# Two row tiles cast first and transposed in bfloat16 on TensorE, with a new plan of the first ten units

## The chip, the cores and the metric

The kernel runs on one core of a Trainium2 chip. The metric is the device time of one execution in microseconds. Most executions agree within 0.3%, and the times here are medians. A ratio compares two kernels in the same rounds, so it is not quite the ratio of the medians beside it; its 95% interval stands in brackets. A profile is one execution, and its span is some 2 us shorter than the time.

## The reference

```python
def reference(x, w1, w2):            # x: 16 x 512 x 1024, w1 and w2: 1024 x 768, float32
    y1 = np.matmul(x, w1)
    y2 = np.matmul(x, w2)
    return (np.tanh(y1) * y2).astype(np.float32)
```

The 8192 rows of x are 64 row tiles of 128. A matmul needs each row tile transposed, with the 1024 columns on the partitions.

## The kernel before

The first six row tiles, "the head", are multiplied in bfloat16 while the weights are still arriving. The other 58 tiles form 29 pairs. Each pair is multiplied with each weight ("a unit", 58 of them) in float16 by seven products of half-size blocks in place of eight; a product is four matmuls of 384 columns, p1 to p7. Tiles of the pairs are transposed by DMA, tiles of the head on TensorE.

```python
    def pe_transpose_f(mt, h):                       # float32, half a tile
        for k in range(KH):
            pin(nc.tensor.transpose(banks[6 + h][:, k * P:(k + 1) * P],
                                    hf[mt][:, (h * KH + k) * P:(h * KH + k + 1) * P], ident))

    def evacuate_f(mt, h, eng):                      # PSUM float32 -> SBUF bfloat16, half a tile
        ...
    def pe_transpose_b(mt, bank):                    # bfloat16, a whole tile: half the PSUM bytes
        b = bank.bitcast(bf16)
        for k in range(KO):
            pin(nc.tensor.transpose(b[:, k * P:(k + 1) * P], hb[mt][:, k * P:(k + 1) * P], ident_b))
```

The start and the first ten units follow a fixed plan: one list of names per engine, and each engine works its list strictly in order. In the names, `T` is a transpose, `e` its evacuation (the copy from PSUM, where TensorE writes, to SBUF), `hx` the cast of a head tile, `m20F3` the 512-column matmul of tile 2 with weight 0 (w1) and slice 3 (`G`: the other 256 columns), `ca3`/`cb3` the cast of slice 3 of w1/w2, `ax`, `rx`, `cx`, `Tx` the absolute-sum, scale, cast and DMA transpose of a tile of a pair, `s1` to `s4` sums of blocks of x and `t1` to `t4` sums of blocks of a weight, `seed` a copy between two PSUM banks, and `p5.0` product 5 of unit 0. From unit 10 on, a formula gives each operation its place.

```python
    for mt in range(4):
        for h in range(2):
            op(f"T{mt}{h}", "pe", 0.45, 4.5 + 2.3 * mt + 0.1 * h, [f"Lx{mt}", f"e{mt - 1}{h}" if mt else ""], pe_transpose_f, mt, h)
            op2("e", f"e{mt}{h}", ("dve", "act")[h], ...)
    ...
            at(slot(z - 30 + 4 * h), abs_x, i, h)            # steady part: absolute-sums of a pair
        late = 1.1 * (i == FIRST + 1)
        at(slot(z - 25 + late), scale_x, i)
        for h in range(2):
            at(slot(z - 24 + (1 + h) * late + 4 * h), cast_x, i, h, "dve")
            at(slot(z - 24 + (1 + h) * late + 4 * h), transpose_x, i, h)
```

## Time and profile before

| kernel before | |
|---|---|
| time, median of 4 runs | 316.13 us (315.47 to 316.74) |
| span of the profiled run | 314.2 us |
| TensorE, VectorE, ScalarE busy | 98%, 78%, 73% |
| a product of four 384-column matmuls, start to start | 0.65 us |

The chain of waits and TensorE's timeline stand in the prediction below. What they do not show is why TensorE loses 0.74 us at the handoff. These lines are of VectorE's timeline of the kernel before (start, length, instruction, idle before it and what ended it):

```profile
42.48 0.69 DVE L287 TENSOR_TENSOR o<-o,bank 128x512 f32<-128x512 f32 x1 [1.06 <-PE bank L270]
43.09 0.42 DVE L382 TENSOR_TENSOR s<-xT 128x512 f16<-128x512 f16 x1
...
44.77 1.82 DVE L318 SCALAR_TENSOR_TENSOR t<-wf,wp1r,b 128x1536 f16<-128x1536 f32 x1
```

VectorE sat idle for 1.06 us in front of the last head multiplication, because that needs TensorE's last head group. Sums of x and t1 of w2 (line L318) stood behind it in the list, and the product that needs t1 started at 46.63, when t1 was done.

### The profile page before, as it was taken

The numbers are of one execution on the slowest core, as the hardware profiler recorded it, in microseconds if no ns is written. First come the engines' busy times: TensorE is split into PE (matmuls) and PEld (weight loads), VectorE is DVE, ScalarE is ACT, GpSimd is POOL, SyncE is SP. The second block draws the span as 40 slices with busy tenths as digits, with TensorE's granted clock in tenths as the row PEclk, the third lists the DMA queues.
The fourth block names the chain that finished last, engine by engine and source line by source line (L and its number), as shares of the span: only waits on it lengthen the run. The fifth ranks groups of instructions, "written<-read, shape, count | busy, mean of one in ns | idle before, by whom it ended". The sixth has DMA issues, their size and how long they took to land.

```text
span 314.2 us, 5489 instructions
## 1 busy us (share of the span) xinstructions
PE 307.3 (98%) x1893; PEld 185.6 (59%) x1898; DVE 244.8 (78%) x571; ACT 230.5 (73%) x453; POOL 4.3 (1%) x10
## 2 busy tenths in 40 slices
PE   7999999999999999999999999999999999999995
PEld 5756656666656555555555556555555555555662
DVE  1688988888788778877777887777788777778653
ACT  3798879787888777778777777877777787776552
POOL 0000000000000000000000000000000000000004
PEclk9999999999999999999999999999999999999999
DMA  7999398999999999999999989999998989985322
GB/s 276 407 399 381 78 310 237 271 299 258 290 288 310 297 272 231 228 294 266 285 240 252 273 253 225 291 252 259 253 251 281 260 256 271 237 256 126 144 103 100
DMA packets 82300, 80.59 MB, mean 256 GB/s; under 512 B 63584, under 2 KB 64096, under 8 KB 82272
## 3 DMA queue, kind: packets, MB, share of 16 engines
q1 hardware_dynamic: 81552, 78.46, 88.0%
q10 hardware_dynamic: 720, 1.77, 1.4%
q8 instruction: 15, 0.25, 0.3%
q14 instruction: 13, 0.11, 0.1%
HBM read 39.85 MB, written 25.17 MB: 207 GB/s over the span
## 4 chain that ended last, share of the span: by engine, by line
PE 89%; DMA 8%; DVE 1%; issue 1%; ACT 0%; ACTq 0%; SPq 0%; DVEq 0%
PE bank L401 84%; DMA wf<-in_w_dram 8%; PE bank L267 3%; PE bank L270 2%; DVE t L318 1%; DVE s L382 1%; PE bank L238 0%; DVE o L437 0%; ACT o L283 0%; ACTq L250 0%; SPq L250 0%; ACT junk L260 0%; PE bank L300 0%; DVE o L287 0%; DVE out_r L390 0%
## 5 line engine op out<-in xcount | busy, mean ns | idle before, releaser
L401 PE MATMUL bank<-t,s 128*128 128x384 f16 x696 | 131.5, 326 | 0.4 <-DVE t L318 0.4
L401 PEld LDWEIGHTS <-s 128*128 128x128 f16 x928 | 90.7, 98 | 61.1 <-issue 0.8
L401 PEld LDWEIGHTS <-xT 128*128 128x128 f16 x696 | 68.0, 98 | 46.7 <-issue 0.9
L401 PE MATMUL bank<-b,xT 128*128 128x384 f16 x464 | 93.7, 326 | 0.0
L423 DVE TENSOR_TENSOR c<-bank,u 128x384 f32<-128x384 f32 x58 | 31.9, 553 | 41.1 <-PE bank L401 39.6
L340 ACT ACTIVATE junk<-x_f 128x1024 bf16<-128x1024 f32 x58 | 60.8, 1049 | 2.4 <-DMA x_f<-in_x_dram 2.4
L431 ACT ACTIVATE th<-c,out_r 128x384 f32<-128x384 f32 x58 | 35.3, 609 | 21.1 <-DVE c L423 21.1
L401 PE MATMUL bank<-b,s 128*128 128x384 f16 x232 | 47.0, 326 | 0.0
L401 PE MATMUL bank<-t,xT 128*128 128x384 f16 x232 | 46.9, 325 | 0.0
L418 ACT ACTIVATE u<-bank 128x384 f32<-128x384 f32 x58 | 28.2, 487 | 20.0 <-PE bank L401 19.7
L360 DVE TENSOR_SCALAR x_h<-x_f,pr 128x1024 f16<-128x1024 f32 x55 | 41.0, 746 | 0.2
L431 ACT ACTIVATE th<-bank,out_r 128x384 f32<-128x384 f32 x58 | 33.3, 574 | 6.1 <-PE bank L401 6.1
L414 ACT ACTIVATE bank<-bank 128x384 f32<-128x384 f32 x58 | 27.9, 481 | 12.6 <-DVE o L437 10.0
L437 DVE SCALAR_TENSOR_TENSOR o<-bank,out_r,th 128x384 f32<-128x384 f32 x58 | 35.4, 610 | 2.0 <-PE bank L401 2.0
L423 DVE TENSOR_TENSOR c<-bank,s 128x384 f32<-128x384 f32 x58 | 32.1, 554 | 6.1 <-PE bank L401 5.0
L437 DVE SCALAR_TENSOR_TENSOR o<-c,out_r,th 128x384 f32<-128x384 f32 (+1 forms) x57 | 34.3, 606 | 0.4 <-ACT th L431 0.2
L418 ACT ACTIVATE s<-bank 128x384 f32<-128x384 f32 x58 | 27.9, 482 | 7.3 <-PE bank L401 5.1
L382 DVE TENSOR_TENSOR s<-xT 128x512 f16<-128x512 f16 x58 | 24.0, 416 | 0.2
L267 PE MATMUL bank<-wb,xTb 128*128 128x512 bf16 x91 | 23.6, 379 | 0.1
L270 PE MATMUL bank<-wb,xTb 128*128 128x256 bf16 x96 | 14.6, 273 | 0.1
L260 ACT ACTIVATE junk<-wf 128x768 bf16<-128x768 f32 (+1 forms) x13 | 12.8, 988 | 1.4 <-DMA wf<-in_w_dram 1.2
L267 PEld LDWEIGHTS <-xTb 128*128 128x128 bf16 x96 | 9.3, 99 | 7.5 <-DVE xTb L231 0.3
(49 smaller groups left out, 143.4 us busy)
## 6 DMA issues: line engine op xcount, KB each, us to landing
x_f<-in_x_dram SPq DMA_DIRECT2D x64, 512.0 KB, 5.8
out_dram<-o SPq DMA_DIRECT2D x62, 384.0 KB, 3.6
wf<-in_w_dram SPq DMA_DIRECT2D x12, 384.0 KB, 7.7
wf<-in_w_dram ACTq DMA_DIRECT2D x4, 384.0 KB, 8.5
xT<-x_h SPq DMA_TRANSPOSE x58, 3.7
out_dram<-o SPq DMA_DIRECT2D x3, 192.0 KB, 1.9
out_dram<-o ACTq DMA_DIRECT2D x1, 192.0 KB, 1.9
```

What stands on the lines that cost most here:

```text
L260: pin(nc.scalar.activation(junk[:, :n * N].rearrange("p (k n) -> p k n", n=N), w_f[t][:, k:k + n, :], ACT.Abs, accum_out=asum_w[t][:, j:j ...
L267: pin(nc.tensor.matmul(bank, hx[mt][:, k, :], w_b[t][k][:, :F], start=k == 0, stop=k == KO - 1))
L270: pin(nc.tensor.matmul(bank[:, at_:at_ + G], hx[mt][:, k, :], w_b[t][k][:, F:], start=k == 0 and mt % 2 == 0, stop=k == KO - 1, skip_group ...
L340: pin(nc.scalar.activation(junk[:, :K], xs[HEAD + 2 * i + h], ACT.Abs, scale=2.0 ** -12, accum_out=pair_sum[i][:, h:h + 1]))
L360: pin(nc.vector.tensor_scalar(xh, xs.pop(mt), pair_r[i][:, h:h + 1], None, ALU.mult))
L382: pin((nc.vector if eng == "dve" else nc.gpsimd).tensor_tensor(s, st[i, a], st[i, b], op))
L401: pin(nc.tensor.matmul(bank[:, cols], st[i, a][:, k, :], wt[t][b][:, k, cols], start=start and k == 0, stop=stop and k == KH - 1, skip_gro ...
L414: pin(nc.scalar.activation(ub[u]["b"][:, :Q], ub[u]["a"][:, :Q], ACT.Copy))
L418: pin(nc.scalar.activation(c, ub[u][bank][:, :Q], ACT.Copy))
L423: pin(nc.vector.tensor_tensor(c, ub[u][bank][:, :Q], ub[u][other], ALU.add))
L431: pin(nc.scalar.activation(th, v, ACT.Tanh, scale=rs[i][:, 0, h:h + 1]))
L437: pin(nc.vector.scalar_tensor_tensor(o[:, h, q * Q + cols.start:q * Q + cols.stop], v, rs[i][:, 1, h:h + 1], tanhs[i, h, q][:, cols], ALU. ...
```

## The change

Its intent: on TensorE a bfloat16 transpose costs half of a float32 one (56 against 109 ns from start to start, as the prediction reads it from the trace), so two more of the head's tiles are cast before the transpose; and the plan is made anew around this.

```diff
-    for mt in range(4):
+    for mt in range(2):
         for h in range(2):
             op(f"T{mt}{h}", "pe", 0.45, ..., pe_transpose_f, mt, h)
             ...
+    for mt in (2, 3):
+        op2("hx", f"hx{mt}", "dve", 4.5 + 2.3 * mt, [f"Lx{mt}", "hx2" if mt == 3 else ""], cast_head_x, mt)
+        op(f"T{mt}", "pe", 0.45, 4.6 + 2.3 * mt, [f"hx{mt}", f"e1{mt - 2}"], pe_transpose_b, mt, banks[4 + mt])
+        op2("eb", f"e{mt}1", "dve", 4.7 + 2.3 * mt, [f"T{mt}", "e10" if mt == 2 else "e21"], evacuate_b, mt, banks[4 + mt])
     ... (needs and buffers that name these operations follow)
-    FILL = {"m00F0": 3, "m00F1": 6}
+    FILL = {"T10": 9, "m00G1": 3}
     "pe":                               (the start, the first matmuls with w2, the handoff)
-    T00 T01 m00F0 m00G0 T10 T11 ... m10F0 T20 m10G0 m10G1 m10F1 T21 m20G0 ... T30 T31 m10G3
+    T00 T01 T10 T11 m00G0 m00F0 ... m10F1 T2 m00G2 m00F2 m10F2 m10G2 m20G0 ... m20G2 T3 m10G3
-    ... m00F5 m00F6 m00F7 suma m11F0 m20F6 m20F7 m01F0 ... m30F7 m21F0 m21F1 m11F2 ...
+    ... suma m11F0 m01F0 m31F0 m11F1 ... m01F3 m21G3 m31F3 m11F3 m21F0 m00F3 m00F4 m00F5 m00F6 m00F7 ...
-    ... m51F7 p1.0 p1.1 p5.0 p6.0 p2.0 ...
+    ... m51G5 p1.0 p1.1 p5.0 p5.1 p2.0 p6.0 p6.1 m41G3 m41G4 m41G5 m41G6 m41G7 p7.0 ... m51G6 m51G7 ...
     "act":
-    ... tanh4G ax20 cx11 b11b b22b ...                   u2.8 f01.6 s5.8 cx61 s5.9 seed.9 f10.8 seed.10 ...
+    ... b11b ax20 tanh4G b22b ...                        f11.6 seed.9 f00.8 ... u2.9 s5.10 seed.10 f00.10
     "dve":
-    ... mul4G s1.0 s2.0 s4.0 s3.0 sx1 t1b ...
+    ... t1b s1.0 t2b s2.0 rx2 s3.0 ... mul4G ...
     "dma":
-    ... Lb5 Lb6 Lx5 Lb7 Lp00 ...
+    ... Lb5 Lx5 Lb6 Lp00 Lb7 ...                         (cuts marked by dots; the lists are long)
```

More of the change, by code (lines that the diff above doesn't have):

```diff
@@ L58 @@
     ELSEWHERE = {
-        "e01": "dve", "e11": "dve", "e20": "act", "e21": "dve", "e31": "dve", "ca0": "act", "ca1": "act",
-        "cb4": "act", "b22a": "dve", "cx11": "act", "cx31": "act", "cx61": "act"
+        "e00": "act", "e11": "dve", "ca1": "act", "b22a": "dve", "cx11": "act", "cx31": "act", "cx41":
+        "act", "cx60": "act"
     }
-    FILL = {"m00F0": 3, "m00F1": 6}
+    FILL = {"T10": 9, "m00G1": 3}
     ORDER = {
         "pe": """
-            T00 T01 m00F0 m00G0 T10 T11 m00F1 m00G1 m10F0 T20 m10G0 m10G1 m10F1 T21 m20G0 m20F0 m20F1 m20G1
-            m10G2 m20G2 m00F2 m00G2 m20F2 m10F2 T30 T31 m10G3 m00G3 m20F3 m10F3 m20G3 m00F3 m10F4 m10G4 m20F4
-            m20G4 m00G4 m00F4 m30G0 m30G1 m30G2 m30G3 m20G5 m10G5 m10F5 m20F5 m20G6 m10G6 m10F6 m30G4 m30G5
-            m30G6 m20G7 m10G7 m30G7 m10F7 m00F5 m00F6 m00F7 suma m11F0 m20F6 m20F7 m01F0 m00G5 m00G6 m00G7
-            m11F1 m01F1 m30F0 m30F1 m30F2 m30F3 m30F4 m30F5 m30F6 m30F7 m21F0 m21F1 m11F2 m21F2 m01F2 m11F3
-            m21F3 m01F3 m31F0 m31F1 m31F2 m31F3 m21G0 m21G1 m21G2 m21G3 m31G0 m31G1 m31G2 m31G3 m01F4 m31G4
-            m21G4 m11F4 m01G0 m01G1 m11G0 m11G1 m01G2 m01G3 m01G4 m31F4 T4 m11F5 m11F6 m01F5 m31F5 m01G5 m01G6
-            m31F6 m01F6 m31G5 m31G6 m01F7 m31F7 m11F7 m31G7 T5 m40F0 m40F1 m40F2 m40F3 m40F4 m40F5 m40F6 m01G7
-            m40F7 m21G5 m21G6 m50F0 m50F1 m50F2 m50F3 m50F4 m50F5 m50F6 m50F7 m21F4 m21F5 m21G7 m21F6 m21F7
-            m11G2 m11G3 m11G4 m11G5 m11G6 m11G7 m40G0 m50G0 m50G1 m50G2 m50G3 m50G4 m50G5 m50G6 m50G7 m40G1
-            m40G2 m40G3 m40G4 m40G5 m40G6 m40G7 sumb m41F0 m41F1 m41F2 m41F3 m41F4 m41F5 m41F6 m41F7 m41G0
-            m41G1 m41G2 m41G3 m41G4 m41G5 m41G6 m51G0 m51G1 m51G2 m51G3 m51G4 m51G5 m51G6 m51G7 m41G7 m51F0
-            m51F1 m51F2 m51F3 m51F4 m51F5 m51F6 m51F7 p1.0 p1.1 p5.0 p6.0 p2.0 p3.0 p7.0 p5.1 p6.1 p4.0 p2.1
-            p7.1 p1.2 p3.1 p4.1 p1.3 p6.2 p2.2 p5.2 p6.3 p2.3 p5.3 p7.2 p7.3 p3.2 p4.2 p3.3 p4.3 p1.4 p1.5
-            p5.4 p5.5 p2.4 p6.4 p6.5 p2.5 p7.4 p7.5 p3.4 p3.5 p4.4 p4.5 p1.6 p1.7 p5.6 p6.6 p2.6 p6.7 p2.7
-            p7.6 p3.6 p5.7 p7.7 p4.6 p3.7 p1.8 p4.7 p1.9 p2.8 p6.8 p5.8 p5.9 p7.8 p1.10 p3.8 p4.8 p3.9 p6.9
-            p2.9 p2.10 p7.9 p5.10 p4.9
@@ new lines @@
+            T00 T01 T10 T11 m00G0 m00F0 m00G1 m00F1 m10F0 m10G0 m10G1 m10F1 T2 m00G2 m00F2 m10F2 m10G2 m20G0
+            m20G1 m20F0 m20F1 m20F2 m20G2 T3 m10G3 m00G3 m10F3 m20F3 m20G3 m20F4 m00G4 m20G4 m10G4 m30F0 m30F1
+            m30G0 m30G1 m30G2 m30G3 m30G4 m20F5 m00G5 m10G5 m30G5 m20G5 m20F6 m00G6 m30G6 m20G6 m10G6 m20F7
+            m20G7 m30G7 m00G7 m10G7 m10F4 m10F5 m10F6 m10F7 suma m11F0 m01F0 m31F0 m11F1 m31F1 m01F1 m21G0
+            m21G1 m31G0 m11F2 m31F2 m01F2 m21G2 m01F3 m21G3 m31F3 m11F3 m21F0 m00F3 m00F4 m00F5 m00F6 m00F7
@@ new lines @@
+            m21F1 m21F2 m21F3 m30F2 m30F3 m30F4 m30F5 m30F6 m30F7 T4 m01G0 m01G1 m01G2 m11G0 m11G1 m11G2 m11G3
+            m21F4 m21F5 m11F4 m31F4 m01F4 m01F5 m21G4 m11F5 m31F5 m01G3 m01G4 m01G5 m21F6 m11F6 m31F6 m01F6
+            m01G6 m11G4 m11G5 m11G6 m01F7 m11G7 m21F7 m31F7 m01G7 m11F7 T5 m40F0 m40F1 m40F2 m40F3 m40F4 m40F5
+            m40F6 m40F7 m50F0 m50F1 m50F2 m50F3 m50F4 m50F5 m50F6 m50F7 sumb m40G0 m21G5 m21G6 m21G7 m31G1
+            m31G2 m31G3 m31G4 m31G5 m31G6 m31G7 m41F0 m41F1 m41F2 m40G1 m40G2 m41F3 m41F4 m41F5 m41F6 m41F7
@@ new lines @@
+            m40G3 m40G4 m40G5 m50G0 m40G6 m40G7 m50G1 m50G2 m50G3 m50G4 m50G5 m50G6 m50G7 m51F0 m51F1 m51F2
+            m51F3 m51F4 m51F5 m51F6 m51F7 m41G0 m51G0 m41G1 m41G2 m51G1 m51G2 m51G3 m51G4 m51G5 p1.0 p1.1 p5.0
+            p5.1 p2.0 p6.0 p6.1 m41G3 m41G4 m41G5 m41G6 m41G7 p7.0 p3.0 p7.1 p4.0 m51G6 m51G7 p3.1 p2.1 p4.1
+            p1.2 p1.3 p5.2 p5.3 p2.2 p6.2 p6.3 p2.3 p7.2 p7.3 p3.2 p4.2 p3.3 p4.3 p1.4 p5.4 p1.5 p6.4 p2.4
+            p5.5 p6.5 p2.5 p3.4 p7.4 p7.5 p5.6 p4.4 p3.5 p4.5 p1.6 p1.7 p5.7 p2.6 p6.6 p3.6 p6.7 p2.7 p1.8
@@ L82 @@
+            p7.6 p7.7 p3.7 p4.6 p4.7 p5.8 p5.9 p6.8 p2.8 p3.8 p1.9 p7.8 p3.9 p5.10 p4.8 p6.9 p2.9 p1.10 p7.9
+            p2.10 p4.9
         """,
         "act": """
-            ca0 absa0 ca1 absa1 e20 absa2 absa3 absa4 absa5 absa6 absa7 tanh2G absb0 tanh1F tanh0G tanh2F cb4
-            tanh0F absb2 absb6 tanh3F absb4 ax00 absb7 ax01 b21a tanh4F tanh5F ax10 ax11 tanh4G ax20 cx11 b11b
-            b22b seed.0 seed.1 s5.0 u2.0 ax21 b21b u2.1 f00.0 s5.1 f10.0 ax31 seed.2 ax30 seed.3 f11.0 u2.2
@@ L87 @@
-            u2.3 s5.2 s5.3 f00.2 f01.0 ax40 cx31 f10.2 seed.4 ax41 seed.5 s5.4 s5.5 u2.4 u2.5 f11.2 f00.4 ax51
-            f01.2 ax50 f10.4 seed.6 f11.4 seed.7 f01.4 u2.6 s5.6 ax61 u2.7 s5.7 f00.6 f11.6 f10.6 seed.8 ax60
-            f00.8 u2.8 f01.6 s5.8 cx61 s5.9 seed.9 f10.8 seed.10 u2.9 f01.8 f11.8 f00.10 s5.10
+            e00 e01 ca1 absa1 absa0 absa2 absa3 absa4 absa5 absa6 absa7 tanh2G tanh0G tanh2F tanh1F absb0 b21a
+            tanh0F absb2 tanh3F absb4 ax00 absb6 ax01 absb7 tanh4F ax10 tanh5F ax11 b11b ax20 tanh4G b22b ax21
@@ L90 @@
+            seed.0 seed.1 s5.0 cx11 u2.0 u2.1 s5.1 b21b f00.0 f10.0 ax30 ax31 seed.2 seed.3 f01.0 ax40 u2.2
+            f11.0 u2.3 s5.2 s5.3 ax41 f00.2 f10.2 cx31 seed.4 s5.4 seed.5 ax51 u2.4 u2.5 f01.2 f11.2 s5.5 cx41
+            s5.6 f00.4 f01.4 f10.4 seed.6 ax50 seed.7 f00.6 f11.4 u2.6 u2.7 s5.7 ax60 ax61 f01.6 f10.6 seed.8
+            s5.8 cx60 u2.8 s5.9 f11.6 seed.9 f00.8 f01.8 f11.8 f10.8 u2.9 s5.10 seed.10 f00.10
         """,
         "dve": """
-            e00 e01 e10 e11 ca2 e21 ca3 ca4 e30 ca5 ca6 e31 ca7 parta cb0 cb1 scalea b11a cb2 cb3 t1a b22a hx4
@@ L93 @@
-            cb6 cb5 t2a e41 cb7 hx5 mul0F mul3F mul1F e51 t3a rx0 cx00 cx01 mul2G mul2F mul0G partb t4a rx1
-            cx10 scaleb mul4F sx0 mul4G s1.0 s2.0 s4.0 s3.0 sx1 t1b t2b t3b c22.0 rx2 sx2 cx20 t4b s1.1 c22.1
-            f00.1 s2.1 c12.0 f10.1 s3.1 cx21 c12.1 s4.1 f11.1 rx3 cx30 c22.2 c22.3 s3.2 s1.2 f00.3 f01.1 c12.2
-            c12.3 s2.2 f10.3 mul5F rx4 cx40 s4.2 cx41 s3.3 c22.4 f11.3 c22.5 f00.5 s1.3 c12.4 f01.3 s2.3 f10.5
-            rx5 f11.5 s4.3 cx50 c12.5 f01.5 c22.6 sx3 cx51 c22.7 f00.7 s1.4 s2.4 sx4 s3.4 c12.6 c12.7 rx6 cx60
@@ L98 @@
-            s4.4 sx5 f01.7 c22.8 f10.7 f11.7 s1.5 s2.5 c12.8 s3.5 c12.9 f00.9 c22.9 s4.5 f11.9 f01.9 f10.9
+            ca0 e10 e11 hx2 ca2 e21 hx3 ca3 ca4 e31 ca5 ca6 ca7 parta cb0 cb1 scalea cb2 cb3 b11a b22a hx4 cb5
+            cb4 t1a t2a cb6 e41 cb7 hx5 mul0F mul1F e51 rx0 mul2F cx00 partb t4a scaleb cx01 mul2G mul3F mul4F
+            rx1 mul0G cx10 t1b s1.0 t2b s2.0 rx2 s3.0 sx0 t3a s4.0 t3b c22.0 cx20 c22.1 t4b c12.0 f00.1 f10.1
+            s1.1 c12.1 cx21 s2.1 f01.1 s4.1 rx3 s3.1 cx30 f11.1 c22.2 c22.3 sx1 s1.2 c12.2 s2.2 f00.3 c12.3
@@ L99 @@
+            f10.3 rx4 s4.2 sx2 s3.2 mul4G cx40 mul5F s1.3 c12.4 c22.4 f11.3 sx3 c22.5 f01.3 f00.5 c12.5 s2.3
+            f01.5 f10.5 s4.3 rx5 s3.3 cx50 f11.5 cx51 c12.6 c22.6 c22.7 sx4 s1.4 c12.7 s2.4 s3.4 rx6 s4.4
+            f10.7 f00.7 f01.7 c12.8 s1.5 c22.8 f11.7 cx61 s3.5 s2.5 sx5 s4.5 f00.9 c12.9 c22.9 f11.9 f01.9
+            f10.9
         """,
         "dma": """
-            Lx0 La0 Lx1 La1 Lx2 La2 Lx3 La3 La4 La5 La6 La7 Lb0 Lb1 Lb2 Lb3 Lb4 Lx4 Lb5 Lb6 Lx5 Lb7 Lp00 Lp01
-            Lp10 Lp11 Tx00 Lp20 Tx01 st3 Lp21 Tx10 Lp30 st4 Tx11 Lp31 st1 Tx20 Lp40 Lp41 Tx21 st2 Lp50 Tx30
@@ L103 @@
-            Lp51 Tx31 Lp60 st5 Tx40 Lp61 st0 Tx41 Lp70 store1.5 Tx50 store0.5 Lp71 Tx51 store0.1 store1.1 Tx60
-            store0.7 store1.7 Tx61 store1.3 store0.3 store0.9 store1.9
+            Lx0 La0 Lx1 La1 Lx2 La2 Lx3 La3 La4 La5 La6 La7 Lb0 Lb1 Lb2 Lb3 Lb4 Lx4 Lb5 Lx5 Lb6 Lp00 Lb7 Lp01
+            Lp10 Lp11 Tx00 Lp20 Tx01 Lp21 st1 Lp30 Tx10 Lp31 Tx11 Lp40 st0 Tx20 Lp41 st2 Tx21 Lp50 Tx30 Lp51
+            store1.1 Tx31 Lp60 st4 Tx40 st5 Lp61 Tx41 Lp70 store0.5 st3 Tx50 store1.5 store0.1 Tx51 Lp71 Tx60
@@ L105 @@
+            store0.7 store1.7 Tx61 store0.3 store1.3 store0.9 store1.9
         """,
@@ L547 @@
                 op(f"abs{a}{k}", "act", 0.23 + 0.82 * n, 8 + 1.3 * k + 17 * t, [f"L{a}{k + n - 1}"], abs_w, t, k, n)
-    held = {6: "e30", 7: "e31"}
+    held = {6: "e21", 7: "e31"}
     def accumulate(m, t, which, bank, due):
@@ L555, in accumulate @@
             for k in range(KO):
-                needs = [f"c{'ab'[t]}{k}", f"e{mt}{k // KH if mt < 4 else 1}",
+                needs = [f"c{'ab'[t]}{k}", f"e{mt}{k // KH if mt < 2 else 1}",
                          f"m{mt}{t}{which}{k - 1}" if k else f"m{m}{t}G0" if n else held.get(bank, "")]
@@ L592 @@
            load_head_x, mt)
-        op2("hx", f"hx{mt}", "dve", 28 + 2 * n, [f"Lx{mt}", f"hx{mt - 1}" if n else ""], cast_head_x, mt)
+        op2("hx", f"hx{mt}", "dve", 28 + 2 * n, [f"Lx{mt}", f"hx{mt - 1}"], cast_head_x, mt)
         op(f"T{mt}", "pe", 0.45, 27 + 2.5 * n, [f"hx{mt}", held.get(5, "")], pe_transpose_b, mt, banks[5])
-        op2("eb", f"e{mt}1", "dve", 27.5 + 2.5 * n, [f"T{mt}", "e30" if n == 0 else ""], evacuate_b, mt, banks[5])
+        op2("eb", f"e{mt}1", "dve", 27.5 + 2.5 * n, [f"T{mt}", f"e{mt - 1}1"], evacuate_b, mt, banks[5])
         held[5] = f"e{mt}1"
@@ L598 @@
             scales(1, 5, 36)
+    if HEAD == 4:
+        scales(1, 5, 36)
     for m in (0, 2):
@@ L627 @@
             r = HEAD + n - 6
-            x_free = f"e{r}1" if r < 4 else f"hx{r}" if r < HEAD else f"cx{(r - HEAD) // 2}{r % 2}"
-            h_free = f"Tx{(n - 4) // 2}{n % 2}" if n >= 4 else f"T{HEAD - 4 + n}" if HEAD - 4 + n >= 4 else ""
+            x_free = "" if r < 0 else f"e{r}1" if r < 2 else f"hx{r}" if r < HEAD else f"cx{(r - HEAD) // 2}{r % 2}"
+            h_free = f"Tx{(n - 4) // 2}{n % 2}" if n >= 4 else f"T{HEAD - 4 + n}"
             op(f"Lp{i}{h}", "dma", 1.35, (21 + n - 200 if n < 2 else 23 + n - 200 if n < 4 else due - 12), [x_free, f"Lp{(n - 1) // 2}{(n - 1) % 2}" if n else f"Lx{HEAD - 1}" if HEAD > 4 else "Lb3"], load_x, HEAD + n)
@@ L633 @@
             op(f"ax{i}{h}", "act", 1.26, due - 8 + h, [f"Lp{i}{h}", f"ax{i - 1}{h}" if i else ""], abs_x, i, h)
-            op2("cx", f"cx{i}{h}", "dve", due - 5 + h, [f"rx{i}", f"cx{(n - 1) // 2}{(n - 1) % 2}" if n else f"hx{HEAD - 1}" if HEAD > 4 else "", h_free],
+            op2("cx", f"cx{i}{h}", "dve", due - 5 + h, [f"rx{i}", f"cx{(n - 1) // 2}{(n - 1) % 2}" if n else f"hx{HEAD - 1}", h_free],
                cast_x, i, h)
-            t_need = [f"Tx{(n - 1) // 2}{(n - 1) % 2}"] if n else [f"e{HEAD - 1}1" if HEAD > 4 else "e30"]
+            t_need = [f"Tx{(n - 1) // 2}{(n - 1) % 2}"] if n else [f"e{HEAD - 1}1"]
             if n >= 10 - HEAD:
```

## The prediction

> **What bounds the kernel now.** I read the page first, then the chain that ended last in order of time, then the TensorE timeline from 0 to 66 us, and last the VectorE, ScalarE and DMA-issuing timelines beside it.
>
> The page:
>
> ```profile
> span 314.2 us, 5489 instructions
> PE 307.3 (98%) x1893; PEld 185.6 (59%) x1898; DVE 244.8 (78%) x571; ACT 230.5 (73%) x453; POOL 4.3 (1%) x10
> PEclk9999999999999999999999999999999999999999
> PE 89%; DMA 8%; DVE 1%; issue 1%; ACT 0%; ACTq 0%; SPq 0%; DVEq 0%
> ```
>
> TensorE is the bound: busy 98% of the span, never throttled, 89% of the chain. The chain, in order of time, shows where it is not:
>
> ```profile
> 16.95 8.61 DMA wf<-in_w_dram
> 27.08 0.91 PE bank L270 x7
> 43.09 0.43 DVE s L382
> 44.83 1.77 DVE t L318
> 46.63 263.86 PE bank L401 x1612
> ```
>
> So there is a start that waits for weights, a stage from about 27 us in which TensorE works off its queue, a handoff near 43 to 46 us where VectorE leads, and then 264 us of nothing but products (1612 in 263.86 us, 164 ns each). The change touches only the first three. The instruction orders of the two builds agree from the end backwards as far as the last 1337 matmuls; everything after the first ten units is the same program.
>
> The TensorE timeline of the start and of the handoff (start, length, instruction, idle before it):
>
> ```profile
> 6.21 1.06 PE L223 MATMUL bank<-ident,x_f 128*128 128x128 f32 x8 [1.18 <-DMA x_f<-in_x_dram]
> 8.27 1.09 PE L223 MATMUL bank<-ident,x_f 128*128 128x128 f32 x8 [0.15 <-DMA x_f<-in_x_dram]
> 10.52 0.66 PE L223 MATMUL bank<-ident,x_f 128*128 128x128 f32 x4 [0.18 <-DMA x_f<-in_x_dram]
> 11.45 0.60 PE L223 MATMUL bank<-ident,x_f 128*128 128x128 f32 x4
> 13.51 1.04 PE L223 MATMUL bank<-ident,x_f 128*128 128x128 f32 x8
> 14.38 0.38 PE L270 MATMUL bank<-wb,xTb 128*128 128x256 bf16 x2
> 28.04 0.61 PE L238 MATMUL bank<-ident_b,x_b 128*128 128x128 bf16 x8
> 28.49 1.03 PE L267 MATMUL bank<-wb,xTb 128*128 128x512 bf16 x4
> 43.94 1.66 PE L401 MATMUL bank<-b,xT 128*128 128x384 f16 x8
> 45.44 0.81 PE L401 MATMUL bank<-t,s 128*128 128x384 f16 x4
> 46.63 0.81 PE L401 MATMUL bank<-t,s 128*128 128x384 f16 x4 [0.38 <-DVE t L318]
> ```
>
> The length of a row contains the latency of its last matmul, so I take costs from start to next start. Eight float32 transposes: 13.51 to 14.38, 0.87 us, 109 ns each. Eight bfloat16 transposes: 28.04 to 28.49, 0.45 us, 56 ns each. In the same way a 512-column head matmul is 216 ns, a 256-column one 109 ns and a product of four 384-column matmuls 0.65 us. Up to 10.5 us TensorE follows the arrival of row tiles 0, 1 and 2 (idle time ends with a DMA three times). From 14.38 to 43.94 the planned order adds up, at those costs and with 0.23 us for each of the two sums, to 29.6 us, and it took 29.56: that stage has no bubble. At the handoff eight products' matmuls take 1.50 instead of 1.30 (0.20 lost), and four take 1.19 instead of 0.65 (0.54 lost, to the VectorE block that makes t1 of the second weight). So 0.74 us is lost there and under 1 us at the start; nothing else in the touched part is to be had except the transposes themselves.
>
> **What the Trainium skill says.** (1) "TensorE: Matmul & The Clock Gate", section "Wait — 56ns, not 53.3ns?": warm matmuls start every N/2.4 GHz plus about 2.5 ns, 55.6 ns at 128 columns and 215.7 at 512. The trace agrees for bfloat16: 56 and 216. (2) Same page, "Part 4: PE-mode transpose": a transpose lands in PSUM and needs a VectorE copy after, and it is given about 275 ns in context; here 109 and 56 ns start to start count, since they are pipelined. (3) "VectorE: DVE Perf Modes", "Mode 2×_2P — use both read ports for one tensor": a single-source operation from SBUF gets two elements a cycle even in float32, but PSUM has one read port. The trace agrees: 128x1024 float32 cast from SBUF 0.69 us, 128x512 float32 evacuated from PSUM also 0.69, half the rate; a 128x1024 bfloat16 evacuation from PSUM takes 0.69. (4) "Perfetto Trace Analysis", "Roofline": a lone core is bounded by its 16 DMA engines at about 435 GB/s. The trace moves 399 to 416 GB/s from 5 to 30 us, so loads arrive as fast as they can, and their order is what counts.
>
> **The change part by part.**
>
> *Transposes.* 16 float32 transposes become 16 bfloat16: 16 x (109 - 56) = 0.85 us less on TensorE. But each tile now waits for load, cast (0.69), transpose, evacuation (0.69), where before only load, transpose, evacuation stood in line. The VectorE work is nearly equal: of tile 2 and 3 it had three float32 evacuations of 0.69 (ScalarE had one of 0.59), now two casts and two evacuations, 2.76 us against 2.07.
>
> *The start, by hand.* Tile 0 and 1 keep float32. From the trace: x0 lands 6.1, x1 8.2, x2 10.5, x3 12.75, w1's slices a1 8.8, a2 11.05, a3 13.25, a4 13.95. Tile 1's transposes now come before any matmul of tile 0, so those end at 9.20, then 0.33 of matmuls, three fillers, 0.65 and 0.32 more: TensorE is dry at about 10.85. The nine earlier fillers lie in the wait for x1 and cost nothing. The cast of tile 2 runs 10.52 to 11.21, so its transposes run 11.28 to 11.73: 0.43 idle. Then four matmuls of slice 2 (0.65) to 12.40; tile 2's evacuation runs from about 11.93 to 12.62, so 0.28 idle; six matmuls (0.97) to 13.65; tile 3's cast (12.79 to 13.48) is ready, transposes to 14.10. At that point exactly the work is done that stood done at 14.38 before: three tiles times three slices and all transposes. So of the 0.85 saved, 0.28 remain; the rest goes into waits for cast and evacuation.
>
> *The middle.* Two loads change place: the last-but-one and the last slice of w2 come after row tile 5 and after the first steady tile, each about 1.3 us later (25.6 to 26.9 and 27.8 to 29.1, since a 512 KB tile takes 1.3 us in that stream). Walking TensorE's new order from 14.10 at the costs above, the first matmul of the one stands at 29.2 and of the other at 30.5, and the casts should be done at 28.8 and 29.9. No stall, margins of 0.4 to 0.6.
>
> *The handoff.* Before, the first sums of x stood behind the last head multiplication on VectorE, and t1 of w2 behind those, which cost the 0.74. Now t1 of w2 stands before them, and five head matmuls plus two are kept back to fill between products. My walk of VectorE puts t1 at 41.5 to 43.3 against its product at about 44.9. So the 0.74 should go.
>
> *What it adds.* ScalarE now has the tanh of the last 256-column head group behind the absolute-sum of steady tile 4 (its third pair). That tile's load is issued behind the first DMA transpose, which waits for the first scaled cast (35.0 by my walk, 35.3 before), so at about 36.4; before it took 4.25 us (36.75 to 41.0). So it lands about 40.65, its sum is done about 41.85, the tanh about 42.45, and the bank that the tanh frees is wanted by TensorE at 42.0. That is a new stall of about 0.5.
>
> *Sum.* 0.28 at the start + 0.74 at the handoff - 0.5 for the tanh = 0.5 us less. The filler count (9 to 12) is inside waits. I take another 0.0 to 0.3 for casts that I placed too early.
>
> **The rivals.** *All of it counts:* transposes give the full 0.85 and the handoff 0.74: 1.6 us, 314.6. For it: TensorE is the bound and dense. Against it: x2 lands at 10.5 whatever is done, and the cast now stands between. *The longer chain eats everything:* cast, transpose and evacuation leave TensorE waiting as long as the saving, and the tanh wait eats the handoff: 316.2, no change. For it: the idle times before 10.5 us are all DMA. Against it: the handoff loss is real and its cause is moved. *A new wait in the first ten units:* VectorE is 4.6 to 4.9 us busy of 5 in several stretches from 20 to 40 us, so one late cast (of the last w2 slice, say) delays everything behind it by 0.5 to 1 us: 316.5 to 317. For it: margins under 0.6 us. Against it: TensorE's new order holds the dependent matmuls back. The steady part has two bubbles of 0.15 (near 91 and 105 us), just after the planned units; they may go or double, worth 0.3 either way.
>
> **Range and chances.** 316.16 - 0.5 = 315.66; as the tanh wait is the least certain term and could vanish, I shade it to 315.6. The three runs before spread by 1.3 us, so a median of a few runs is good to about 0.4; with the terms above the range is 314.5 to 316.8. A change of 2% is 6.3 us; all that the change can reach (start and handoff losses plus the transposes) is under 3, so faster by 2% is practically excluded, 0.01. Slower by 2% would need a stall of several microseconds that no queue shows: 0.02. Within 2%: 0.97.
>
> **What would show it.** Right: eight bfloat16 transposes of tile 2 starting near 11.3 and of tile 3 near 13.65, the next head matmul at about 14.1; the first product near 43.5; no wait of a product for the t block of w2; an idle of up to 0.5 of TensorE before a 256-column head matmul near 42, released by ScalarE; TensorE's last matmul about 0.5 earlier than before. Wrong: TensorE dense through 10.8 to 11.3 (then the cast was hidden and the gain is nearer 1 us), a hole near 29 to 31 us in front of the matmuls of the last w2 slices, or DMA transposes of the first pair landing after 43.

## The result, and the profile after

The changed kernel took 316.20 us (median of 4 runs, 315.81 to 316.36), the kernel before 316.13 in the same rounds: ratio 1.0001 [0.9979, 1.0023]. Six more runs in a later job gave 315.97, ratio 0.9996 [0.9979, 1.0012]. The time lies in the predicted range, which is 2.3 us wide, but of the predicted 0.5 us nothing can be seen. Neither interval alone excludes it (0.5 us is a ratio of 0.9984); all ten runs of the changed kernel average 316.15, all fifteen of the kernel before 316.20. So the question is where each term went.

The page of the changed kernel:

```profile
span 314.3 us, 5503 instructions
PE 307.2 (98%) x1901; PEld 185.2 (59%) x1901; DVE 243.8 (78%) x571; ACT 231.7 (74%) x453; POOL 4.3 (1%) x10
PE 86%; DMA 9%; DVE 2%; ACT 1%; ACTq 0%; issue 0%; SPq 0%; DVEq 0%
```

TensorE is as busy as before, but its share of the chain fell from 89% to 86%, with 9% on DMA. The chain in order of time says where the others broke in:

```profile
12.61 8.66 DMA wf<-in_w_dram
21.29 0.57 DVE wb L255
21.91 0.38 PE bank L268
...
36.30 4.58 DMA x_f<-in_x_dram
40.96 1.15 ACT junk L341 x2
42.11 0.49 ACT o L284
42.65 1.14 PE bank L271 x9
43.79 4.55 PE bank L402 x28
...
90.12 0.48 DVE c L424
90.60 0.22 ACT junk L341
90.81 0.39 ACT bank L415
91.25 219.32 PE bank L402 x1340
```

There are three breaks. A slice of w2 lands at 12.61 + 8.66 = 21.27, is cast, and TensorE goes on with it at 21.91. A row tile lands at 40.88, ScalarE sums it, then does a tanh (L284), and TensorE goes on at 42.65. At 90 us ScalarE ends a sum (L341), copies a bank (L415), and TensorE goes on at 91.25. TensorE's own timeline shows how long it stood:

```profile
9.68 0.38 PE L268 MATMUL bank<-wb,xTb 128*128 128x512 bf16 x1
10.25 0.62 PE L239 MATMUL bank<-ident_b,x_b 128*128 128x128 bf16 x8 [0.18 <-DVE x_b L218]
...
12.64 0.61 PE L239 MATMUL bank<-ident_b,x_b 128*128 128x128 bf16 x8
13.08 0.38 PE L271 MATMUL bank<-wb,xTb 128*128 128x256 bf16 x2
...
18.32 0.81 PE L268 MATMUL bank<-wb,xTb 128*128 128x512 bf16 x3
19.94 0.81 PE L268 MATMUL bank<-wb,xTb 128*128 128x512 bf16 x3 [0.81 <-DVE wb L255]
...
25.90 0.61 PE L239 MATMUL bank<-ident_b,x_b 128*128 128x128 bf16 x8
...
40.26 1.89 PE L268 MATMUL bank<-wb,xTb 128*128 128x512 bf16 x8
42.65 1.14 PE L271 MATMUL bank<-wb,xTb 128*128 128x256 bf16 x9 [0.50 <-ACT o L284]
43.63 1.46 PE L402 MATMUL bank<-b,xT 128*128 128x384 f16 x8
```

As in the prediction, I count from start to start: 9.68 to 10.25 is 0.57 where a 512-column matmul takes 0.216, so 0.35 is lost to the cast of tile 2. From 18.32 to 19.94 is 1.62 where three take 0.65, so 0.97 is lost to a slice of w2. From 40.26 to 42.65 is 2.39 where eight take 1.73, so 0.67 is lost to the tanh. All starts in this profile look some 1 us early against the kernel before: its first row tile landed at 5.03 us, there at 6.07. The experiments show that this is the run, not the kernel: the kernel before had it at 5.01 in its second profile, and two programs with the same start, run on the same chip ("both" and "tanh first" below), had it at 5.01 and 5.74.

**Lateness.** One number helps to compare profiles. Take the start of the n-th product matmul (n from 0) and subtract n x 0.1625 us, a quarter of a product's 0.65. The result stays constant while TensorE runs product after product, and a hole adds its length. At n = 120 the handoff is over and all head matmuls are done. The two places where it then jumps in most profiles are n = 284 (288 in the old plan; unit 10, near 90 us) and n = 372 (unit 13, near 105 us). From n = 400 to the last matmul it grows by 1.3 to 1.5 in every profile. All starts and landings used here are read from the traces.

| profile | n=120 | n=360 | n=400 | last matmul |
|---|---|---|---|---|
| before | 44.68 | 44.87 | 45.03 | 46.41 |
| before, again | 44.13 | 44.33 | 45.53 | 46.98 |
| changed | 44.39 | 45.09 | 45.09 | 46.49 |
| changed, again | 44.11 | 44.81 | 44.81 | 46.21 |
| transposes alone | 44.14 | 44.33 | 44.62 | 46.00 |
| plan alone | 44.28 | 44.98 | 45.06 | 46.47 |
| tanh first | 43.60 | 44.30 | 44.30 | 45.70 |
| sum behind seed | 43.87 | 44.03 | 44.32 | 45.78 |
| both | 43.65 | 43.80 | 44.26 | 45.65 |
| tanh first + w1 first | 43.13 | 43.83 | 43.83 | 45.17 |
| + sum behind seed | 43.58 | 43.74 | 44.28 | 45.76 |
| + earlier cast | 43.18 | 43.95 | 44.00 | 45.43 |
| + split casts | 43.62 | 44.39 | 44.45 | 45.87 |

Each row is one run, and a run can lie off its kernel's median: "sum behind seed" was profiled at 315.53 (median 316.27), "tanh first + w1 first" at 314.77 (315.46), "+ sum behind seed" at 315.69 (315.21). The runs of the experiments also come from three jobs, each on another chip. So the table shows where time was lost in a run; which kernel is faster is a matter for the medians and ratios.

Between the first profiles of the two kernels the changed one is 0.29 ahead when the handoff is over. By n = 400 it is 0.06 behind: near 90 us it lost 0.70 where before lost 0.19, and near 105 us nothing where before lost 0.16. That is the account of this pair of profiles; the experiments say which parts of it repeat. In the second pair the changed kernel is only 0.02 ahead at n = 120, and 0.77 at the last matmul.

### The profile page after: what moved, and what is told of

The parts are those of the page before. It is cut to its first block, busy times and chain, and to the rows that moved or that the text cites. A ratio compares the mean times of both kernels' runs of the same rounds, so it can differ in the third digit from the quotient of the medians.

```text
span 314.3 us, 5503 instructions
## 1 busy us (share of the span) xinstructions
PE 307.2 (98%) x1901; PEld 185.2 (59%) x1901; DVE 243.8 (78%) x571; ACT 231.7 (74%) x453; POOL 4.3 (1%) x10
## 3 DMA queue, kind: packets, MB, share of 16 engines
q10 hardware_dynamic: 720, 1.77, 1.4%
## 4 chain that ended last, share of the span: by engine, by line
PE 86%; DMA 9%; DVE 2%; ACT 1%; ACTq 0%; issue 0%; SPq 0%; DVEq 0%
PE bank L402 81%; DMA wf<-in_w_dram 6%; PE bank L268 3%; DMA x_f<-in_x_dram 3%; PE bank L271 1%; DVE o L438 1%; DVE c L424 1%; ACT junk L341 0%; ACTq L251 0%; DVE s L383 0%; PE bank L239 0%; DVE wb L255 0%; ACT th L432 0%; ACT o L284 0%; ACT u L419 0%
## 5 line engine op out<-in xcount | busy, mean ns | idle before, releaser
L341 ACT ACTIVATE junk<-x_f 128x1024 bf16<-128x1024 f32 x58 | 60.8, 1049 | 2.3 <-DMA x_f<-in_x_dram 2.1
L361 DVE TENSOR_SCALAR x_h<-x_f,pr 128x1024 f16<-128x1024 f32 x54 | 40.3, 745 | 0.0
L415 ACT ACTIVATE bank<-bank 128x384 f32<-128x384 f32 x58 | 27.9, 481 | 10.7 <-DVE o L438 8.1
L268 PE MATMUL bank<-wb,xTb 128*128 128x512 bf16 x96 | 24.8, 379 | 0.9 <-DVE wb L255 0.8
```

The source lines that it names most:

```text
L268: pin(nc.tensor.matmul(bank, hx[mt][:, k, :], w_b[t][k][:, :F], start=k == 0, stop=k == KO - 1))
L341: pin(nc.scalar.activation(junk[:, :K], xs[HEAD + 2 * i + h], ACT.Abs, scale=2.0 ** -12, accum_out=pair_sum[i][:, h:h + 1]))
L361: pin(nc.vector.tensor_scalar(xh, xs.pop(mt), pair_r[i][:, h:h + 1], None, ALU.mult))
L415: pin(nc.scalar.activation(ub[u]["b"][:, :Q], ub[u]["a"][:, :Q], ACT.Copy))
```

## The experiments

Each kernel ran six times (the last two: five), with eleven runs of the kernel before in the same job; "before, again" ran once. All gave correct results.

### 1. The changed kernel and the kernel before, once more

No edit.

> The changed kernel once more, for a closer interval and a second look at its start. In its first profile the first row tile landed at 5.03 us, in the kernel before at 6.07, and the changed kernel then waited 0.98 us for the second slice of w2. Theory A (the start is luck of the run, the two cancel): ratio to before within 0.998 to 1.002, and the landing of the first tile differs again by some tenths to 1 us between this profile and the first, while TensorE reaches the transposes of tile 4 at 25.9 in either. Rival B (the change itself makes the loads start earlier): it lands at 5.0 again and the 0.98 us wait for w2 is there again.

Measured: 315.97, ratio 0.9996 [0.9979, 1.0012]. The first tile landed at 5.56, not 5.03, and the wait for the second slice of w2 was 0.37, not 0.97; tile 4's transposes started at 25.92, in the first profile at 25.90. Theory A.

> The kernel before unchanged, for a second look. Theory A (the landing of the first tile is luck, the old plan is not bound by w2's slices): first tile at another time than 6.07, between 5.0 and 6.1, tile 4's transposes follow the first tile's landing and not w2's fourth slice; hole of 0.74 at the handoff again and lateness near 90 to 105 us of 0.3. Rival B: tile 4's transposes at the same distance (6.71) from w2's fourth slice as in the first profile.

Measured: 316.58, one run; first tile at 5.01, tile 4's transposes at 27.33 where they had been at 28.04. The distance to w2's fourth slice is 6.16, not 6.71: the old plan is not tied to that slice, and rival B falls. The handoff again lost time (0.91). But my 0.3 for 90 to 105 us was wrong by far: TensorE's timeline of this profile of the kernel before shows

```profile
104.13 0.81 PE L401 MATMUL bank<-b,xT 128*128 128x384 f16 x4
105.97 0.81 PE L401 MATMUL bank<-t,xT 128*128 128x384 f16 x4 [1.03 <-DVE c L423]
```

and VectorE's timeline of the same stretch

```profile
104.22 0.42 DVE L382 TENSOR_TENSOR s<-xT 128x512 f16<-128x512 f16 x1 [1.16 <-DMA xT<-x_h]
...
105.36 0.55 DVE L423 TENSOR_TENSOR c<-bank,s 128x384 f32<-128x384 f32 x1
```

The product waits 1.19 us for an addition (c, at 105.36), which stands on VectorE behind two sums of pair 7 and another addition; the first of these sums waits for the DMA transpose of row tile 21. It landed at 104.20; in the first profile of before at 103.69, with a hole of 0.14. So the same program has a hole of 0.14 or of 1.19 us there. The earlier start of this profile was more than given back.

### 2. The tanh ahead of the sum

```diff
-  ... ax11 b11b ax20 tanh4G b22b ...      (ScalarE's list)
+  ... ax11 b11b tanh4G ax20 b22b ...
```

> The tanh of the last head group is put ahead of the absolute-sum of steady tile 4 on ScalarE; nothing else. Theory A (ScalarE's order makes the 0.67 us hole near 42 us, and TensorE is the bound after it): the hole before the 256-column matmul near 42 us goes, TensorE's last matmul comes 0.5 to 0.7 us earlier, time 315.6. Rival B (the hole hides a later wait, for the DMA transposes of the first pair or for the boundary near 90 us): the hole goes but another of 0.3 us or more opens before 50 us or grows near 90 us, time 316.1 to 316.3.

Measured: 315.69, ratio to before 0.9980 [0.9966, 0.9994]. TensorE's timeline at the same place as above:

```profile
40.12 1.89 PE L268 MATMUL bank<-wb,xTb 128*128 128x512 bf16 x8
41.85 1.15 PE L271 MATMUL bank<-wb,xTb 128*128 128x256 bf16 x9
```

1.73 for eight: the hole is gone, and nothing opens later; the holes after n = 120 are those of the changed kernel. Theory A. In the profiles of the new plan that keep the sum in front of the tanh, the matmul began 1.77 us after that row tile landed: 42.65 after 40.88, 42.36 after 40.59, 42.12 after 40.35, and 42.54 after 40.77 in "plan alone". The hole was 0.67, 0.36, 0.43 and 0.43. Against the changed kernel of the same job the median fell from 315.97 to 315.69; the intervals of the two ratios overlap.

### 3. The sum behind the seed copy, alone and with the tanh

```diff
-            at(slot(z - 30 + 4 * h), abs_x, i, h)
+            at(slot(z - 30 + 4 * h + 1.2 * (i == FIRST + 1 and h == 1)), abs_x, i, h)
```

The changed kernel has the sum of row tile 21 in front of the seed copy of unit 10 on ScalarE; this swaps the two and nothing else.

> One absolute-sum of row tile 21 (second tile of steady pair 7) goes behind the seed copy of unit 10 on ScalarE; the planned units are untouched. Theory A (the 0.71 us hole near 90 us is only that order): hole down to under 0.1 us, time 315.5 to 315.6. Rival B (the slack of the whole steady schedule is set there: the delayed sum delays its cast and its transpose): the hole is moved to 95 to 110 us, time 316.0 or more.

> Both ScalarE moves. Theory A (TensorE is the bound and the two holes are separate): gains add, 1.2 to 1.4 us, time 314.8 to 315.0, ratio to before near 0.996. Rival B (the second hole follows from the first): no more than the better of the two alone, 315.5.

Measured: alone 316.27, 0.9995 [0.9980, 1.0011]; with the tanh 315.81, 0.9985 [0.9970, 1.0000], no better than the tanh alone. The hole near 90 did fall, from 0.71 to 0.17 in both; TensorE's timeline of "sum behind seed":

```profile
89.36 0.81 PE L402 MATMUL bank<-t,s 128*128 128x384 f16 x4
90.15 0.81 PE L402 MATMUL bank<-b,xT 128*128 128x384 f16 x4
```

The four matmuls took 0.79 to the next start (1.36 in the changed kernel, to 91.25), where other products take 0.65; 0.03 more is lost in the next four. But one of 0.29 and 0.46 opened near 105: rival B of the first entry, at the place it named. Of the second entry neither theory held as put: the 90 us hole does not follow from the one at 42, yet the gains do not add, because a third limit stands behind.

### 4. The two parts apart

Transposes alone: the plan of before with the new operations, where only the matmuls around them change place.

```diff
-  ... m10F0 T20 m10G0 m10G1 m10F1 T21 m20G0 ... m20F2 m10F2 T30 T31 m10G3 ...
+  ... m10F0 m10G0 m10G1 m10F1 T2 m10G2 m00F2 m00G2 m10F2 m20G0 ... m20F2 T3 m10G3 ...
-  e00 e01 e10 e11 ca2 e21 ca3 ca4 e30 ca5 ca6 e31 ca7      (VectorE)
+  e00 e01 e10 e11 hx2 ca2 e21 hx3 ca3 ca4 e31 ca5 ca6 ca7
```

> The plan of before, with row tiles 2 and 3 cast first and transposed in bfloat16; only the matmuls around those transposes change place. Theory A (the transposes buy what is left after the wait for the cast): TensorE idle about 0.4 before the transposes of tile 2 and 0.3 after, everything of the head 0.2 to 0.3 us earlier than in before at the same landing of the first tile, the hole of 0.74 at the handoff near 44 to 46 us still there, time 315.7 to 316.1. Rival B (the float32 transposes cost their full 0.85 on the path): 315.2. Rival C (the longer chain costs more than it saves): 316.4 or more.

Measured: 315.66, ratio 0.9990 [0.9969, 1.0012]; the six runs spread from 314.91 to 316.62, so the time alone decides nothing; its median lies just under the 315.7 of theory A. TensorE's timeline:

```profile
10.22 0.38 PE L266 MATMUL bank<-wb,xTb 128*128 128x512 bf16 x1
10.87 0.62 PE L237 MATMUL bank<-ident_b,x_b 128*128 128x128 bf16 x8 [0.27 <-DVE x_b L216]
...
13.26 0.61 PE L237 MATMUL bank<-ident_b,x_b 128*128 128x128 bf16 x8
13.71 0.38 PE L269 MATMUL bank<-wb,xTb 128*128 128x256 bf16 x2
```

0.43 is lost before tile 2's transposes and, further on, 0.30 before the matmuls that need its evacuation. The clean measure, free of the luck of the start, is from the landing of row tile 2 to the first matmul after tile 3's transposes: 3.62 us here, 3.90 in the first profile of before. So by this pair of profiles bfloat16 is worth 0.28 and not 0.85. (The second profile of before gives 4.27, because its first eight transposes took 213 ns each in place of 109.) The handoff lost 0.88. Theory A in its mechanism.

Plan alone: the new lists, with float32 transposes `T20 T21` and `T30 T31` in place of `T2` and `T3`, and their four evacuations in place of casts and evacuations.

> The new plan, with float32 transposes for row tiles 2 and 3. In the five profiles of the new plan the transposes of tile 4 start 4.62 to 4.63 us after the landing of w2's fourth slice, whenever the first tile landed (5.0 to 5.7). Theory A (in the new plan TensorE waits for w2's slices, and nothing won before 20 us counts): tile 4's transposes again 4.6 to 4.7 after that landing, time as the changed kernel, 315.9 to 316.2. Rival B (the bfloat16 transposes are what the new plan gains by): tile 4's transposes 0.2 to 0.9 later against the landing, time 316.2 to 317.

Measured: 316.14, ratio 1.0007 [0.9991, 1.0023]. Landing of tile 2 to the first matmul after the transposes: 3.78 against 3.61 to 3.62 in the changed kernel. Even those 0.17 do not count, as the chain of this profile shows:

```profile
12.10 9.30 DMA wf<-in_w_dram
...
21.43 0.57 DVE wb L255
...
22.04 0.38 PE bank L268
```

w2's fourth slice lands at 21.40 and TensorE takes it up at 22.04. Tile 4's transposes come at 26.03, again 4.63 after the landing. In the five earlier profiles of the new plan it was 4.62 or 4.63, while the first tile landed anywhere from 5.01 to 5.74. Theory A: in the new plan TensorE waits at 19 to 22 us for slices of w2, and what was won before is lost there.

### 5. Work that needs no w2 goes first

To the tanh move is added:

```diff
-  ... suma m11F0 m01F0 ... m21F0 m00F3 m00F4 m00F5 m00F6 m00F7 m21F1 ...
+  ... suma m00F3 m00F4 m00F5 m00F6 m00F7 m11F0 m01F0 ... m21F0 m21F1 ...
```

> The kernel with the tanh moved ahead (315.69), and in addition the five last 512-column matmuls of row tile 0 with w1, which need nothing more from memory, before the first matmuls with w2 and not after them. Theory A (the waits for w2's second and fourth slice lose what the start wins): no wait for a cast of w2 between 18 and 22 us, tile 4's transposes 3.8 to 4.5 after the landing of the fourth slice, the head 0.2 to 0.8 earlier, time 315.2 to 315.5. Rival B (the last slices, at 26.7 and 29 us, or the transposed first pair at 41.6 bound it anyway): a wait opens at 29 to 31 or before the first product, time 315.6 to 315.8.

Measured: 315.46, ratio 0.9982 [0.9966, 0.9997]. TensorE's timeline:

```profile
18.93 2.53 PE L267 MATMUL bank<-wb,xTb 128*128 128x512 bf16 x11
21.30 0.49 PE L270 MATMUL bank<-wb,xTb 128*128 128x256 bf16 x3
...
25.30 0.61 PE L238 MATMUL bank<-ident_b,x_b 128*128 128x128 bf16 x8
```

Eleven matmuls take 2.37, without a wait, and tile 4's transposes come 4.25 after the fourth slice. Lateness at n = 120 falls to 43.13, 0.47 less than with the tanh alone (a run of another job), and none of it is lost again in this profile. In the profile of experiment 6, with the same order, 0.33 of it is: there TensorE waited at 28.8 to 29.1 us for the cast of w2's seventh slice, near where rival B put a wait. The mechanism is theory A's. The gain in time over the tanh move is not resolved: 0.9982 here and 0.9980 there, from two jobs.

### 6. The third limit

To this is added the swap of experiment 3.

> The kernel with the tanh ahead and w1's last matmuls first (315.46), and in addition the absolute-sum of row tile 21 behind the seed copy. In the nine profiles so far, wherever TensorE waited near 104 to 106 us, the waiting product began 1.77 us after the landing of tile 21's DMA transpose. Theory A (that landing is a second gate, with 0.35 us of slack in the kernel without this edit): the hole near 90 falls from 0.70 to about 0.15, a hole of 0.2 to 0.4 opens near 104 at 1.77 after that landing, time 315.1 to 315.4. Rival B (the holes are independent): no hole near 104, time 314.8 to 315.0.

Measured: 315.21, ratio 0.9976 [0.9962, 0.9989], the best median, but not resolved from the 0.9980 and 0.9982 before it. Theory A, with a larger hole than its 0.2 to 0.4: tile 21's transpose landed at 102.95, and the product started at 104.72, 1.77 later, after a hole of 0.53. VectorE's and TensorE's lines, from the timeline of all engines:

```profile
102.97 0.42 DVE L382 TENSOR_TENSOR s<-xT 128x512 f16<-128x512 f16 x1 [0.43 <-DMA xT<-x_h]
...
104.11 0.55 DVE L423 TENSOR_TENSOR c<-bank,s 128x384 f32<-128x384 f32 x1
...
104.72 0.81 PE L401 MATMUL bank<-t,xT 128*128 128x384 f16 x4 [0.36 <-DVE c L423]
```

The same distance in the other profiles with such a hole: 105.97 after 104.20, 105.46 after 103.69, 105.06 after 103.29, 104.70 after 102.93. A hole of 0.07 in the profile of "plan alone" is another: it came 2.17 after the landing, and VectorE did not wait for the transpose there. (That the distance equals the 1.77 of experiment 2 is chance; other operations stand in between.) In the changed kernel the landing at 103.40 allowed 105.17 and TensorE came at 105.54, so this limit slept behind the hole at 90, with 0.37 to spare.

Then the cast and the transpose of row tile 21 are moved one place earlier:

```diff
-            at(slot(z - 24 + (1 + h) * late + 4 * h), cast_x, i, h, "dve")     (transpose_x the same)
+            at(slot(z - 24 + (1 + h) * late + 4 * h - early * h), cast_x, i, h, "dve")   # early = 2.2 for pair 7
```

> As w1_sum, and the scaled cast of row tile 21 and its DMA transpose come one place earlier in the steady schedule. Theory A (the landing of tile 21's transpose is the gate): it lands 0.5 us or more earlier, the hole near 104 is under 0.1, time 314.8 to 315.0. Rival B (the earlier cast holds up the additions behind it on VectorE, or the transpose lands no earlier, since loads and stores share the DMA engines): a new hole of 0.2 or more between 92 and 106, time 315.2 or more.

Measured: 315.29, ratio 0.9977 [0.9964, 0.9990]. The transpose landed at 100.12 and the hole near 105 is gone, as theory A has it; but holes of 0.26 and 0.35 opened at 95 and 98 us, as rival B has it. TensorE's timeline:

```profile
94.04 0.81 PE L401 MATMUL bank<-b,xT 128*128 128x384 f16 x4
94.95 0.81 PE L401 MATMUL bank<-t,xT 128*128 128x384 f16 x4
...
96.90 0.81 PE L401 MATMUL bank<-b,s 128*128 128x384 f16 x4
97.90 1.30 PE L401 MATMUL bank<-t,s 128*128 128x384 f16 x7 [0.19 <-ACT u L418]
```

Four matmuls took 0.91 and 1.00 in place of 0.65. Each operation moved out of one way stood in another.

### 7. The casts in two halves

```diff
+            if mt < 4:
+                for c in (slice(0, K // 2), slice(K // 2, K)):
+                    pin(nc.vector.tensor_copy(hb[mt][:, c], hf[mt][:, c]))
```

> As w1_sum_cast, and the casts of row tiles 2 and 3 are each done in two halves, so that the first four transposes wait for half a cast. Theory A (what remained of the 0.85 saved was lost in the wait for cast and evacuation): the 0.37 idle before tile 2's transposes falls to 0.1 to 0.2, the first matmul after tile 3's transposes comes 3.3 to 3.5 us after the landing of row tile 2 and not 3.61, time 0.1 to 0.3 less than w1_sum_cast. Rival B (the two halves cost as much as they win, or tile 2's evacuation, which waits for w1's third slice's cast, stays where it is): 3.55 to 3.65, no gain.

Measured: 315.54, ratio 0.9982 [0.9970, 0.9994]. TensorE's timeline:

```profile
10.35 0.38 PE L272 MATMUL bank<-wb,xTb 128*128 128x512 bf16 x1
10.66 0.73 PE L243 MATMUL bank<-ident_b,x_b 128*128 128x128 bf16 x8
...
28.27 0.49 PE L275 MATMUL bank<-wb,xTb 128*128 128x256 bf16 x3
29.17 1.02 PE L272 MATMUL bank<-wb,xTb 128*128 128x512 bf16 x4 [0.40 <-DVE wb L259]
```

The wait before tile 2's transposes fell to 0.10 as expected, and the distance from the landing of tile 2 from 3.61 to 3.46: the wait for the cast did eat part of the saving. The time did not follow: TensorE waited 0.57, from 28.6 to 29.2, for the cast of w2's seventh slice. The slice itself had landed at 27.12; VectorE's timeline shows what held the cast back:

```profile
25.84 1.81 DVE L323 SCALAR_TENSOR_TENSOR t<-wf,wp0r,b 128x1536 f16<-128x1536 f32 x1
27.69 0.96 DVE L327 TENSOR_TENSOR t<-b,t 128x1536 f16<-128x1536 f16 x1
28.56 0.55 DVE L259 CAST wb<-wf 128x768 bf16<-128x768 f32 x1
```

The cast stands behind two blocks t of w1, and these behind the casts of w2's fifth and sixth slices. In the four profiles with w1 first it began 3.69 us after the landing of the sixth slice, which came at 24.87 here and at 24.43 in the run without the split. That difference arises in the stream of loads and not in the edit; the run of experiment 6 had it at 24.84 without a split, and its wait of 0.33. This says again that work won before the stream of loads ends is worth only what the stream allows.

## Why the prediction was right or wrong

**Right: the worth of the transposes.** It worked out 0.43 and 0.28 of waiting and 0.28 of gain from the 0.85. Measured with whole casts: waits of 0.25 to 0.43 and 0.29 to 0.30, and a gain of 0.28 in the old plan (0.17 in the new). The split cast of experiment 7 shows that the wait is for the cast. A slip beside it: VectorE's 2.76 us for these tiles against 2.07 is called nearly equal, and is a third more.

**Right: the handoff.** The 0.74 lost there is gone in all profiles of the new plan: from n = 0 to n = 120 lateness grows by 0.76, which is the seven head matmuls of 109 ns kept back as filling. The t1 of w2 ran from 41.44 to 43.25, where the prediction put 41.5 to 43.3. The old order lost 0.74, 0.91 and 0.88 in its three profiles.

**Right in kind, run-dependent in size: the tanh behind the sum.** It said 0.5; the profiles show 0.67, 0.36, 0.43 and 0.43. The order on ScalarE is the cause, as experiment 2 shows. Taking it away gained 0.3 us by the medians and 0.5 by the ratios 0.9980 and 0.9996.

**Wrong: "The middle. ... No stall, margins of 0.4 to 0.6."** I followed only the two late slices of w2 that change place. The slices that bind are the second and the fourth, because the new plan starts on w2 earlier and leaves w1 work for after. TensorE waited 0.97 and 0.23 us for them in the first profile, and 0.37 and 0.09 in the second. By the prediction's own costs the fourth slice was due: it landed at 21.33 before, with a cast of 0.55, and the same walk, continued from 14.10, puts its first matmul at 21.8. I had not looked. The two late slices themselves caused no stall in either profile, as predicted. So the 0.28 of the start is not kept.

**Mis-sized: the two bubbles near 91 and 105 us.** The prediction gave them 0.15 each, "worth 0.3 either way". The first became 0.71, since the new plan leaves a sum in front of the seed copy on ScalarE (sum at 89.65, copy at 90.69; in the kernel before the copy at 89.04 and the sum at 90.30). So "everything after the first ten units is the same program" failed at the seam: the orders agree only for the last 1337 of the 1624 product matmuls, from n = 287, and the hole is at 284. The second is 0.14 or 1.19 in the kernel before itself. It is not a small steady bubble but a wait for one DMA transpose, whose landing moves from run to run. A single profile could not tell that. This is why the handoff's gain does not show reliably at the end: in the first pair of profiles 0.29 was won by n = 120 and all of it lost by n = 400; in the second pair 0.02 became 0.77, by the hole of 1.19 in the kernel before. That the time still fell in the range is owed to the range's width, not to the sum of terms.

**The rivals.** "All of it counts" (314.6) fell by experiment 4. "The longer chain eats everything" (316.2) named the time that came, but not the mechanism: the chain left 0.28. The tanh took 0.36 to 0.67 of the handoff's 0.74, as this rival has it in part; what ate the rest lay elsewhere. "A new wait in the first ten units" was the nearest in kind; the waits came at 19 to 22 us and just behind the planned units.

What stays open is why tile 21's transpose lands late. It took 5.3 to 8.0 us from issue to landing where the median of all 58 is 3.7 to 4.2, while loads of pair 9 and stores are in flight. That these share the DMA engines fits, but no run took them away. Nor did a run test the fillers.

## What to carry to other kernels

Before you count what a cheaper operation saves, look at what its input waits for: here a cast put in front gave back two thirds of the saving as idle time. Where data arrive in a stream, walk every first use of every slice, not only of those that the change moves; work that needs nothing more from memory belongs in front of the first use of what is still under way. And profile an unchanged kernel twice: a hole that is 0.14 us in one run and 1.19 in the next is a race between two chains, and it decides whether a gain upstream reaches the end.

## What the Trainium skill lacked or had wrong

- "TensorE: Matmul & The Clock Gate", "Part 4: PE-mode transpose": gives about 275 ns for a bfloat16 transpose in a kernel's context, and has no figure for float32 and none for back-to-back transposes. Here a 128x128 bfloat16 transpose is listed with a length of 219 ns and starts 56 ns after the one before it; a float32 one is listed with 273 and takes 109 from start to start (213 for the first eight of one profile).
- "DMA: Bandwidth & Descriptors", "Latency and other measured facts": gives DMA transposes a bandwidth of 261 GB/s (350 to 400 in the contiguous case), by which a 256 KB tile would move in about 1.0 us (an estimate from the 261), and a fixed cost of about 2 us for any DMA, but no time from issue to landing under load. Here that was 3.0 us at best, 3.7 to 4.2 in the median and up to 8.0.
- No page has how a full stream of loads varies from run to run: the first row tile landed between 5.01 and 6.07 us, and w2's third slice between 20.0 and 20.6 in all thirteen profiles, whichever the first had been.
- No page has the time from the landing of a slice to the first matmul with its cast: 0.64 us here (21.27 to 21.91), of which the cast is listed with 0.57.
